# A decoder block's MLP in two sweeps: seven products each for the up and the down projection, factors kept in device memory

## The chip, the cores and the metric

The kernel runs on one core of a Trainium2 chip. The metric is the device time of one launch, in microseconds, as the median of several runs; the profile is one more execution of the same program with the hardware profiler on.

## The reference

One decoder layer on a sequence of 512 tokens, model width 2048, all float32. A first part (delta-rule heads, differential attention, output projection, residual) is the same in both kernels. The change is in the MLP that follows it, cut to what matters:

```python
h = h + jnp.einsum("bse,ed->bsd", mix, w_o[l])
u = rms_norm(h, mlp_norm[l])                                   # 512 x 2048
hid = jnp.square(jax.nn.relu(jnp.einsum("bsd,df->bsf", u, w_up[l])))   # w_up 2048 x 8192
h = h + jnp.einsum("bsf,fd->bsd", hid, w_down[l])              # w_down 8192 x 2048
return rms_norm(h, final_norm)
```

## The kernel before

**Three matmuls for one.** Every float32 operand is split into a high part (rounded to fp32r by ScalarE, line 147 in `parts`) and a low part (the rest, by VectorE, line 149), and a product is the sum of high x high, high x low and low x high. A weight tile of 128 x 1024 elements is one unit: one ScalarE instruction, one VectorE instruction, then TensorE's matmuls. The high and low tiles live in two rings of 3 buffers (`hi`, `lo`), the loaded weights in a ring `raw` of 6.

**Blocks.** The hidden width 8192 is cut in 16 blocks of 512. The up projection of a block is plain: `cols_steps` makes 16 k-steps x 4 column groups x 3 = 192 matmuls of 512 moving columns (lines 204 to 206; block 0 by `up_first`, lines 978 to 980). Its result passes relu and square on ScalarE (lines 965, 966).

**Down in seven products.** The down projection of blocks 0 to 14 is done with Strassen's scheme in Winograd's form on halves of the tokens, of the block's rows and of the output columns: seven products instead of eight. `seven_steps` makes the seven left factors of a block out of the activations (sums, then a split by `two`, 512 elements per partition each); `block_steps` makes the weight sums t1 to t4 in place with VectorE (lines 864, 870, 878, 884), splits them, and calls `product` (lines 835 to 837): 12 matmuls of 512 columns for each of the seven products and each of two column halves `p`, 168 for a block. After every product VectorE adds the PSUM result to the rows of the residual `h`, which stays in SBUF (lines 850, 852). The last block's down projection is plain (192 matmuls).

**Order.** Down of block b is woven with up of block b + 1 and b + 2 and with the factors of block b + 1. The program text is a stream of instructions; a list scheduler of the framework then orders them on each engine, so that an instruction that is ready goes ahead of one that isn't. All weight loads go through SyncE's queue in one chain.

Of the kernel before, what the change touches and what calls it, by code (L numbers as in the profile page):

```python
# [12 lines left out]
F32 = mybir.dt.float32  # L13
F32R = mybir.dt.float32r
AF = mybir.ActivationFunctionType
# [16 lines left out]
def hybrid_block(ctx: ExitStack, tc: tile.TileContext, x, attn_norm, w_in, conv_w, a_log, dt_bias,  # L32
# [758 lines left out]
    weave(chain(attn_values(1, dv[1]), attn_cols(2, df[2]), attn_cols(3, df[3])), att)  # L791


    def half_tile():

        return big("p", [P, 2, 2, 256], nm="hf")

    def two(src):
        z = big("w", [P, 2, 2, 256], F32R, nm="op")
        A.activation(z[:, 0], src, AF.Copy)  # L800
        V.tensor_sub(z[:, 1], src, z[:, 0].bitcast(F32))
        return z[:, 0], z[:, 1]

    def seven_steps(left, f):

        a11, a21, a12, a22 = left[0][:, 0], left[0][:, 1], left[1][:, 0], left[1][:, 1]
        f["a12"] = two(a12)
        yield
        f["a11"] = two(a11)
        z = big("m", [P, 2, 2, 256], nm="s12")  # L810
        s1, s2 = z[:, 0], z[:, 1]
        V.tensor_add(s1, a21, a22)
        yield
        f["s1"] = two(s1)
        V.tensor_sub(s2, s1, a11)
        yield
        f["s2"] = two(s2)
        s4 = s1
        V.tensor_sub(s4, a12, s2)
        yield  # L820
        f["s4"] = two(s4)
        s3 = s2
        V.tensor_sub(s3, a11, a21)
        yield
        f["s3"] = two(s3)
        yield
        f["a22"] = two(a22)
        yield

    def product(bank, fac, wts, first, last_):  # L830
        (ah, al), (bh, bl) = fac, wts
        for k in range(2):
            for t in range(2):
                st = slice(t * P, (t + 1) * P)
                T.matmul(bank[t], lhsT=ah[:, k, st], rhs=bh[:, k, :], start=first and k == 0, stop=False, skip_group_check=True)  # L835
                T.matmul(bank[t], lhsT=ah[:, k, st], rhs=bl[:, k, :], start=False, stop=False, skip_group_check=True)  # L836
                T.matmul(bank[t], lhsT=al[:, k, st], rhs=bh[:, k, :], start=False, stop=last_ and k == 1, skip_group_check=True)  # L837

    def block_steps(f, w, row0, rows):

        for p in range(2):
            def quarter(i, j):
                r0, c0 = row0 + 256 * i, 1024 * j + 512 * p
                return load_w(w[r0:r0 + 256, c0:c0 + 512].rearrange("(k p) n -> p k n", p=P), [P, 2, 512])

            def add(bank, half, cg, op=ALU.add):
                for t in range(2):
                    dst = rows[2 * half + t][cg]
                    if op == ALU.add:
                        V.tensor_add(dst, bank[t], dst)  # L850
                    else:
                        V.tensor_sub(dst, dst, bank[t])

            b21, b11, b12, b22 = quarter(1, 0), quarter(0, 0), quarter(0, 1), quarter(1, 1)
            Y = [bank(), bank()]
            product(Y, f["a12"], parts(b21, 2), True, True)
            add(Y, 0, p)
            yield
            X = [acc(), acc()]
            product(X, f["a11"], parts(b11, 2), True, False)  # L860
            add(X, 0, p)
            yield
            t1 = b11
            V.tensor_sub(t1, b12, b11)
            Z = [acc(), acc()]
            product(Z, f["s1"], parts(t1, 2), True, False)
            add(Z, 1, p + 2)
            yield
            t2 = t1
            V.tensor_sub(t2, b22, t1)  # L870
            product(X, f["s2"], parts(t2, 2), False, False)
            add(X, 0, p + 2)
            yield
            product(Z, f["s4"], parts(b22, 2), False, True)
            add(Z, 0, p + 2)
            yield
            t3 = b12
            V.tensor_sub(t3, b22, b12)
            product(X, f["s3"], parts(t3, 2), False, True)
            add(X, 1, p)  # L880
            add(X, 1, p + 2)
            yield
            t4 = b21
            V.tensor_sub(t4, t2, b21)
            Y = [bank(), bank()]
            product(Y, f["a22"], parts(t4, 2), True, True)
            add(Y, 1, p, ALU.subtract)
            yield


    mixT = {}
# [52 lines left out]
    run(rows_steps(po, w_o[0], 3 * 512, 512, mix, by_token=4, done=finish))  # L944


    def up_unit(u):
# [4 lines left out]
    uT = to_feature_major(h, rstd, g_mlp)  # L952
    NBLK = DFF // 512

    def up_steps(b, j, left):
        z = half_tile()
        for k in range(2):
            po = sps()
            yield from cols_steps(po, w_up[0], (4 * b + 2 * j + k) * P, uT, tag="x")
            squared_relu(z, k, po)  # L960
        left.append(z)

    def squared_relu(z, k, po):
        r = big("m", [P, 512], nm="relu")
        A.activation(r, po, AF.Relu)
        A.activation(z[:, :, k, :], r.rearrange("p (i s) -> p i s", i=2), AF.Square)

    def up_first():

        po = [acc() for _ in range(4)]  # L970
        for u in range(KD // 2):
            hi, lo = up_unit(u) if u else first
            for j in range(2):
                k = 2 * u + j
                ah, al = uT[k]
                for c in range(4):
                    st = slice(c * P, (c + 1) * P)
                    T.matmul(po[c], lhsT=hi[:, j, st], rhs=ah, start=k == 0, stop=False)
                    T.matmul(po[c], lhsT=hi[:, j, st], rhs=al, start=False, stop=False)
                    T.matmul(po[c], lhsT=lo[:, j, st], rhs=ah, start=False, stop=k == KD - 1)  # L980
        for j in range(2):
            z = half_tile()
            for k in range(2):
                squared_relu(z, k, po[2 * j + k])
            lefts[0].append(z)

    def up(b, j):
        return up_steps(b, j, lefts[b]) if b < NBLK else iter(())

    lefts = [[] for _ in range(NBLK)]  # L990
    facs = [{} for _ in range(NBLK)]
    up_first()
    floor.clear()
    run(seven_steps(lefts[0], facs[0]))
    run(up(1, 0))
    for b in range(NBLK - 2):
        down = block_steps(facs[b], w_down[0], 512 * b, h)
        for p in range(2):
            ups = up(b + 1, 1) if p == 0 else up(b + 2, 0)
            fac = seven_steps(lefts[b + 1], facs[b + 1]) if p == 1 else iter(())  # L1000
            for i in range(7):
                next(down)
                next(fac, None)
                if i % 2 == 0:
                    next(ups, None)
            run(ups)


    down = block_steps(facs[NBLK - 2], w_down[0], 512 * (NBLK - 2), h)
    ups = up(NBLK - 1, 1)  # L1010
    for i in range(7):
        next(down)
        if i % 2 == 0:
            next(ups, None)
    run(ups)
    lft = lefts[NBLK - 1]
    fac = [[two(lft[j][:, i]) for i in range(2)] for j in range(2)]
    wts = {}

    def plain_steps(t):  # L1020
        for cg in range(4):
            po = bank()
            for j in range(2):
                if (cg, j) not in wts:
                    r0 = 512 * (NBLK - 1) + 256 * j
                    wts[cg, j] = split(w_down[0, r0:r0 + 256, cg * 512:(cg + 1) * 512].rearrange("(k p) n -> p k n", p=P),
                                       [P, 2, 512], ("u", "u"))
# [83 lines left out]
```

## Time and profile before

| | |
|---|---|
| median of 3 runs | 2282.8 us (2282.29 to 2284.34) |
| the profiled execution's own time | 2282.81 us |
| its span, first to last instruction | 2281.1 us |
| mean granted TensorE clock | 0.997 of full speed |
| one block of the MLP in the steady part | 81.5 us |

The span is the time on the chip from the first to the last instruction; the time of a run has 1.7 us more around it. TensorE matmuls are pipelined: the duration shown for one is longer than the distance to the next one's start, so what a matmul costs in a stream is read from the starts.

### The profile page before, as it was taken

The page shows a single profiled execution, that of the slowest core. Times are in us where ns is not written, and L with a number is a line of the kernel's source. Part 1 is how long each engine was busy: PE and PEld are TensorE (multiplying, and loading weights), DVE is VectorE, ACT ScalarE, POOL GpSimd, SP SyncE. Part 2 cuts the span into 40 slices and gives each one's busy share as a digit, 9 for nine tenths or more (in the row PEclk, how much of TensorE's full clock was granted, in tenths as well). Part 3 has the DMA queues.
Part 4 walks back from the last instruction along what each step waited for, and adds up shares of the span by engine and source line. Part 5 has one row for each costly group of instructions (what it writes and reads, how often), then busy time and mean ns, then how long its engine had stood idle before and what let it go on. Part 6 is the DMA issues. An engine that isn't in the chain of part 4 may idle for free.

```text
span 2281.1 us, 27449 instructions
## 1 busy us (share of the span) xinstructions
PE 2245.4 (98%) x10649; PEld 1864.8 (82%) x10649; DVE 1523.3 (67%) x2338; ACT 887.8 (39%) x1444; POOL 55.5 (2%) x85
## 2 busy tenths in 40 slices
PE   8999999999999999999999999999999999999998
PEld 7988777778888788788888888888888888888887
DVE  5467787863355623437787687777778778777776
ACT  5233434432344523433344343343334334434343
POOL 0000100100000000000000000000000000000000
PEclk9999999999999999999999999999999999999999
DMA  8433333433232434233333333232332333323332
GB/s 282 141 111 95 109 97 96 117 92 110 85 95 88 139 92 151 83 105 98 109 93 119 95 99 113 93 123 90 98 115 93 115 98 95 118 93 120 93 127 95
DMA packets 288570, 249.67 MB, mean 109 GB/s; under 512 B 17300, under 2 KB 229560, under 8 KB 288440
## 3 DMA queue, kind: packets, MB, share of 16 engines
q1 hardware_dynamic: 287952, 247.72, 35.3%
q8 instruction: 83, 1.36, 0.3%
q14 instruction: 47, 0.39, 0.1%
q10 hardware_dynamic: 488, 0.21, 0.0%
HBM read 236.86 MB, written 11.03 MB: 109 GB/s over the span
## 4 chain that ended last, share of the span: by engine, by line
PE 90%; DVE 7%; ACT 1%; issue 1%; DMA 1%; POOL 0%; SPq 0%; ACTq 0%; POOLq 0%; DVEq 0%
PE s L206 10%; PE s L204 10%; PE s L205 10%; PE acc L837 6%; PE acc L836 6%; PE acc L835 6%; PE acc L204 5%; PE acc L205 4%; PE acc L206 4%; PE acc L220 3%; PE acc L221 3%; PE acc L222 3%; PE s L837 2%; PE s L836 2%; PE s L835 2%; DVE X L520 2%
## 5 line engine op out<-in xcount | busy, mean ns | idle before, releaser
L149 DVE TENSOR_TENSOR lo<-raw,hi 128x1024 fp32r<-128x1024 f32 (+2 forms) x370 | 443.9, 1200 | 342.3 <-ACT hi L147 337.5
L147 ACT ACTIVATE hi<-raw 128x1024 fp32r<-128x1024 f32 (+2 forms) x370 | 384.5, 1040 | 674.5 <-PE acc L205 136.7
L204 PE MATMUL s<-u,hi 128*128 128x512 f32 x960 | 373.4, 389 | 0.0
L205 PE MATMUL s<-u,hi 128*128 128x512 f32 x960 | 373.4, 389 | 0.0
L206 PE MATMUL s<-u,lo 128*128 128x512 f32 x960 | 373.4, 389 | 0.0
L149 DVE TENSOR_TENSOR lo<-x,hi 128x1024 fp32r<-128x1024 f32 x120 | 146.7, 1223 | 181.0 <-ACT hi L147 181.0
L204 PE MATMUL acc<-u,hi 128*128 128x512 f32 x640 | 260.6, 407 | 0.8 <-DVE dvl L679 0.6
L205 PE MATMUL acc<-u,hi 128*128 128x512 f32 x640 | 251.6, 393 | 0.0
L206 PE MATMUL acc<-u,lo 128*128 128x512 f32 x640 | 250.7, 392 | 0.0
L147 ACT ACTIVATE hi<-x 128x1024 fp32r<-128x1024 f32 x120 | 127.5, 1062 | 315.0 <-PE s L205 226.2
L836 PE MATMUL acc<-lo,op 128*128 128x512 f32 x600 | 233.4, 389 | 0.0
L837 PE MATMUL acc<-hi,op 128*128 128x512 f32 x600 | 233.4, 389 | 0.0
L835 PE MATMUL acc<-hi,op 128*128 128x512 f32 x600 | 233.1, 389 | 0.0
L850 DVE TENSOR_TENSOR h<-acc,h 128x512 f32<-128x512 f32 x360 | 232.2, 685 | 0.6 <-PE acc L837 0.5
L205 PEld LDWEIGHTS s<-u,hi 128*128 128x128 f32 x960 | 180.2, 188 | 37.4
L206 PEld LDWEIGHTS s<-u,lo 128*128 128x128 f32 x960 | 180.2, 188 | 37.4
L204 PEld LDWEIGHTS s<-u,hi 128*128 128x128 f32 x960 | 180.2, 188 | 37.4
L220 PE MATMUL acc<-hi,u 128*128 128x512 f32 (+2 forms) x384 | 144.7, 379 | 7.6 <-ACT hi L147 5.9
L204 PEld LDWEIGHTS acc<-u,hi 128*128 128x128 f32 x640 | 120.7, 189 | 25.0 <-DVE dvl L679 1.0
L206 PEld LDWEIGHTS acc<-u,lo 128*128 128x128 f32 x640 | 120.4, 188 | 25.3
L221 PE MATMUL acc<-lo,u 128*128 128x512 f32 (+2 forms) x384 | 140.5, 366 | 0.2 <-DVE lo L149 0.2
L222 PE MATMUL acc<-hi,u 128*128 128x512 f32 (+2 forms) x384 | 140.6, 366 | 0.0
(266 smaller groups left out, 3228.2 us busy)
## 6 DMA issues: line engine op xcount, KB each, us to landing
raw<-in_w_down_dram SPq DMA_DIRECT2D x128, 512.0 KB, 5.6
x<-in_w_up_dram SPq DMA_DIRECT2D x120, 512.0 KB, 4.2
raw<-in_w_in_dram SPq DMA_DIRECT2D x96, 512.0 KB, 3.9
raw<-in_w_o_dram SPq DMA_DIRECT2D x32, 512.0 KB, 3.8
raw<-in_w_in_dram SPq DMA_DIRECT2D x16, 384.0 KB, 8.3
w<-in_xt_dram SPq DMA_DIRECT2D x8, 512.0 KB, 8.5
p<-in_x_dram SPq DMA_DIRECT2D x8, 512.0 KB, 10.0
raw<-in_x_dram SPq DMA_DIRECT2D x8, 512.0 KB, 3.6
```

What stands on the lines that cost most here:

```text
L147: A.activation(hi, raw, AF.Copy)
L149: floor["lo"] = V.tensor_sub(lo, raw, hi.bitcast(F32))
L204: T.matmul(po, lhsT=hi[:, j, :], rhs=ah, start=k == 0, stop=False)
L205: T.matmul(po, lhsT=hi[:, j, :], rhs=al, start=False, stop=False)
L206: T.matmul(po, lhsT=lo[:, j, :], rhs=ah, start=False, stop=k == KD - 1)
L220: T.matmul(o, lhsT=ah[:, st], rhs=bh, start=k == 0, stop=False)
L221: T.matmul(o, lhsT=ah[:, st], rhs=bl, start=False, stop=False)
L222: T.matmul(o, lhsT=al[:, st], rhs=bh, start=False, stop=k == KD - 1)
L835: T.matmul(bank[t], lhsT=ah[:, k, st], rhs=bh[:, k, :], start=first and k == 0, stop=False, skip_group_check=True)
L836: T.matmul(bank[t], lhsT=ah[:, k, st], rhs=bl[:, k, :], start=False, stop=False, skip_group_check=True)
L837: T.matmul(bank[t], lhsT=al[:, k, st], rhs=bh[:, k, :], start=False, stop=last_ and k == 1, skip_group_check=True)
L850: V.tensor_add(dst, bank[t], dst)
```

## The change

Up and down become two sweeps. First all 16 blocks are projected up, each of blocks 1 to 15 with seven products too; their down factors are made on the way, and stored to device memory by GpSimd's queue (`keep`). Then the down projection runs over groups of blocks, [0], [1, 2, 3], [4, 5, 6], [7, 8, 9], [10, 11, 12], [13, 14]: the factors of a group are loaded back (`recall`) once and used for both column halves, the blocks of a group accumulate in the same PSUM banks, and the rows of `h` are added to once per product and group. Block 15's down projection stays plain.

- In the up products the weights are the stationary operand and the moving one is a factor of u, 256 columns wide. `u_factors` makes the factors of u once, after `up_first`; for it ScalarE copies each of 16 transposed tiles out of PSUM once more (`uf`).
- `h` is stored to device memory (16 stores on GpSimd's queue) to free its buffers for the factors of u, and loaded back (`rows_back`) at the start of the down sweep.
- The weight sums are made unit by unit beside another product's splits (`sums`, `beside`).
- `raw` has 9 buffers.

```python
-    BUFS = {"p": 10, "x": 2, "w": 8, "m": 2, "u": 16, "raw": 6, "hi": 3, "lo": 3}
+    BUFS = {"p": 10, "x": 2, "w": 8, "m": 2, "u": 16, "raw": 9, "hi": 3, "lo": 3}
...
+    def keep(b, name, src):
+        z = pair_of(src, "w")
+        fscr[b, name] = dp.tile([P, 1024], F32, name=f"f_{name}_{b}")
+        G.dma_start(out=fscr[b, name], in_=z.bitcast(F32).rearrange("p a k s -> p (a k s)"))
...
+    def recall(b, name):
+        z = big("w" if name in ("a12", "a22") else "u", [P, 2, 2, 256], F32R, nm="fac")
+        with tc.issue_after(last_load[0].ins):
+            last_load[0] = nc.sync.dma_start(out=z.bitcast(F32).rearrange("p a k s -> p (a k s)"), in_=fscr[b, name])
+        return z[:, 0], z[:, 1]
+
+    def sums(out, a, b):
+        return [lambda o=o, x1=x1, x2=x2: V.tensor_add(o, x1, x2) for o, x1, x2 in zip(out, a, b)]
...
+        product(X, fa, t1, True, False)                              # block_steps, one group, one p
+        product(Y, fa, t4, True, True, sums(t1, t1, b12))
+        product(Z, fa, t1, True, False, sums(t1, t1, b22))
+        product(X, factor("s2"), t1, False, False)
+        product(Z, factor("s4"), b22, False, True, sums(t4, t4, t1))
+        product(Y, factor("a22"), t4, True, True, sums(b12, b12, b22))
+        product(X, factor("s3"), b12, False, True)
...
+            A.activation(uf[k // 8][k % 8 // 2][:, k % 2], pv, AF.Identity, scale=sc)
+    for cg in range(4):
+        for t in range(NT):
+            G.dma_start(out=hscr[2 * cg + t // 2][:, t % 2, :], in_=h[t][cg])
...
+    def up_product(bank, name, wts, first, last_, beside=()):
+        for n, raw in enumerate(wts):
+            bh, bl = parts(raw, 4)
+            if beside:
+                beside[n]()
+            for j in range(4):
+                k = 4 * n + j
+                ah, al = fu[name][k][:, 0, :], fu[name][k][:, 1, :]
+                for c in range(2):
+                    dst, st = bank[:, c * 256:(c + 1) * 256], slice(c * P, (c + 1) * P)
+                    T.matmul(dst, lhsT=bh[:, j, st], rhs=ah, ...)
+                    T.matmul(dst, lhsT=bh[:, j, st], rhs=al, ...)
+                    T.matmul(dst, lhsT=bl[:, j, st], rhs=ah, ...)
...
+    left = up_first()
+    for b in range(1, NBLK):
+        fac, nxt = seven_steps(b - 1, left), []
+        for _ in up_steps(b, nxt):
+            next(fac, None)
+        run(fac)
+        left = nxt
+    last_fac = four_steps(NBLK - 1, left)
```

`up_steps` of a block makes the seven `up_product`s in the same order as above (a11, a12, s1, s2, s4, a22, s3), with two units per product. Between them ScalarE copies four results out of PSUM (512 elements each), VectorE combines the four quarters of the block (4 instructions of 512), and ScalarE applies relu and square (8 of 512). After each product one step of `seven_steps` of the block before is issued.

## Rows read from the trace of the kernel before

**Rows 1.** The page: the span, and busy time by engine.
```profile
span 2281.1 us, 27449 instructions
PE 2245.4 (98%) x10649; PEld 1864.8 (82%) x10649; DVE 1523.3 (67%) x2338; ACT 887.8 (39%) x1444; POOL 55.5 (2%) x85
```
**Rows 2.** Waits of TensorE from 940 us to the end: total, times, longest.
```profile
PE s L185 <- DVE un L180: 1.2, 1, 1.2
PE s L185 <- ACT un L177: 0.8, 2, 0.5
PE acc L978 <- ACT u L163: 0.3, 1, 0.3
```
**Rows 3.** Windows: one block, two stretches of heavy VectorE, the entry, the kernel's start.
```profile
core 0: us, PE busy (x) PEld busy (x) DVE busy (x) ACT busy (x) POOL busy (x), PEclk, DMA share, GB/s
1600.00:1681.50 81.50, 81.50 (x362) 67.47 (x361) 61.50 (x74) 31.60 (x38) 0.00 (x0) 1.00 0.33 104
...
1641.00:1666.00 25.00, 25.00 (x112) 20.71 (x111) 24.59 (x32) 11.92 (x16) 0.00 (x0) 1.00 0.39 126
...
2160.00:2240.00 80.00, 80.00 (x353) 65.80 (x352) 68.15 (x82) 36.84 (x47) 0.00 (x0) 1.00 0.34 112
...
952.00:964.00 12.00, 10.75 (x70) 8.70 (x71) 9.87 (x20) 11.38 (x21) 0.68 (x1) 1.00 0.16 44
...
20.00:40.00 20.00, 18.49 (x105) 18.17 (x106) 14.39 (x39) 11.69 (x24) 3.03 (x4) 1.00 1.05 391
```
**Rows 4.** Timeline of TensorE: matmuls of 256 columns in attention, of 272, of 512.
```profile
807.06 0.28 PE L734 MATMUL s<-dvl,at 128*128 128x256 f32 x1
...
808.26 0.28 PE L735 MATMUL s<-dvh,at 128*128 128x256 f32 x1
...
87.80 0.29 PE L220 MATMUL acc<-hi,u 128*128 128x272 f32 x1
...
89.94 0.29 PE L222 MATMUL acc<-hi,u 128*128 128x272 f32 x1
...
1704.12 0.39 PE L204 MATMUL s<-u,hi 128*128 128x512 f32 x1
...
1709.33 0.39 PE L206 MATMUL s<-u,lo 128*128 128x512 f32 x1
```
**Rows 5.** Timeline of VectorE, back to back: 1024 elements, and 512.
```profile
1646.93 1.22 DVE L149 TENSOR_TENSOR lo<-raw,hi 128x1024 fp32r<-128x1024 f32 x1
1648.07 1.22 DVE L149 TENSOR_TENSOR lo<-x,hi 128x1024 fp32r<-128x1024 f32 x1
...
1655.28 0.68 DVE L819 TENSOR_TENSOR s<-hf,s 128x512 f32<-128x512 f32 x1
1655.88 1.22 DVE L149 TENSOR_TENSOR lo<-raw,hi 128x1024 fp32r<-128x1024 f32 x1
```
**Rows 6.** The high-part group (by line, ScalarE) in the block of 1600 to 1681.5 us.
```profile
L147 ACT ACTIVATE hi<-raw 128x1024 fp32r<-128x1024 f32 x14 | 14.8, 1057 | 23.0 <-PE s L205 8.3 <-PE acc L837 7.9 <-DVE raw L864 4.9
```
**Rows 7.** Timeline of ScalarE at the MLP's entry.
```profile
954.95 2.40 ACT L163 ACTIVATE u<-s,vec 128x512 fp32r<-128x512 f32 x4
...
964.84 1.12 ACT L147 ACTIVATE hi<-raw 128x1024 fp32r<-128x1024 f32 x1
```
**Rows 8.** DMA issues: KB each, median us to landing.
```profile
raw<-in_w_down_dram SPq DMA_DIRECT2D x128, 512.0 KB, 5.6
...
szscr<-sz SPq DMA_DIRECT2D x4, 512.0 KB, 3.5
```
**Rows 9.** Timelines of GpSimd and VectorE where both work, and one VectorE operation alone.
```profile
165.04 1.40 POOL L460 TENSOR_SCALAR_AFFINE_SELECT pT<-pT 128x1024 f32<-128x1024 f32 x1 [1.63 <-ACT pT L456]
...
164.74 3.02 DVE L415 SCALAR_TENSOR_TENSOR cv<-cv,cw 128x511 f32<-128x511 f32 x3
...
187.94 0.74 DVE L415 SCALAR_TENSOR_TENSOR cv<-cv,cw 128x511 f32<-128x511 f32 x1
```

More of the change, by code (lines that the diff above doesn't have):

```diff
@@ L809, in seven_steps @@
-        f["a11"] = two(a11)
         z = big("m", [P, 2, 2, 256], nm="s12")
         s1, s2 = z[:, 0], z[:, 1]
-        V.tensor_add(s1, a21, a22)
+        keep(b, "a11", a11)
         yield
-        f["s1"] = two(s1)
-        V.tensor_sub(s2, s1, a11)
+        keep(b, "a12", a12)
+        V.tensor_sub(s1, a21, a22)
         yield
-        f["s2"] = two(s2)
-        s4 = s1
-        V.tensor_sub(s4, a12, s2)
+        keep(b, "s1", s1)
+        negated_less(s2, s1, a11)
         yield
-        f["s4"] = two(s4)
@@ L822, in seven_steps @@
-        s3 = s2
-        V.tensor_sub(s3, a11, a21)
+        keep(b, "s2", s2)
         yield
-        f["s3"] = two(s3)
+        negated_less(s1, s2, a12)
+        keep(b, "s4", s1)
         yield
-        f["a22"] = two(a22)
+        keep(b, "a22", a22)
+        V.tensor_add(s2, a11, a21)
         yield
-    def product(bank, fac, wts, first, last_):
-        (ah, al), (bh, bl) = fac, wts
-        for k in range(2):
-            for t in range(2):
[L834 to L888, printed above, removed]
@@ new lines, in seven_steps, with four_steps @@
+        keep(b, "s3", s2)
+        yield
+    def four_steps(b, left):
+        for j in range(2):
+            for i in range(2):
+                keep(b, f"a{i + 1}{j + 1}", left[j][:, i])
+                yield
+    def recall(b, name):
[3 more added lines that the diff above has]
+        return z[:, 0], z[:, 1]
@@ new lines, in sums, with product @@
+    def sums(out, a, b):
+        return [lambda o=o, x1=x1, x2=x2: V.tensor_add(o, x1, x2) for o, x1, x2 in zip(out, a, b)]
+    def product(bank, facs, wts, first, last_, beside=()):
+        for n, ((ah, al), raw) in enumerate(zip(facs, wts)):
+            bh, bl = parts(raw, 2)
+            if beside:
+                beside[n]()
+            for k in range(2):
+                for t in range(2):
+                    st = slice(t * P, (t + 1) * P)
+                    head, tail = first and n == 0 and k == 0, last_ and n == len(facs) - 1 and k == 1
+                    T.matmul(bank[t], lhsT=ah[:, k, st], rhs=bh[:, k, :], start=head, stop=False, skip_group_check=True)
+                    T.matmul(bank[t], lhsT=ah[:, k, st], rhs=bl[:, k, :], start=False, stop=False, skip_group_check=True)
+                    T.matmul(bank[t], lhsT=al[:, k, st], rhs=bh[:, k, :], start=False, stop=tail, skip_group_check=True)
@@ L980, in up_first @@
                     T.matmul(po[c], lhsT=lo[:, j, st], rhs=ah, start=False, stop=k == KD - 1)
+        floor.clear()
+        run(u_factors())
+        left = []
         for j in range(2):
@@ L983, in up_first @@
             for k in range(2):
[L984 to L997, printed above, removed]
-        for p in range(2):
[L999 to L1006, printed above, removed]
@@ L1009, in hybrid_block @@
[L1009 to L1017, printed above, removed]
+                r = big("m", [P, 512], nm="relu")
+                A.activation(r, po[2 * j + k], AF.Relu)
+                A.activation(z[:, :, k, :], r.rearrange("p (i s) -> p i s", i=2), AF.Square)
@@ new lines, in up_first, with u_factors, put @@
+            left.append(z)
+        return left
+    fu = {n: [None] * 8 for n in ("a11", "a12", "a22", "s1", "s2", "s3", "s4")}
+    def u_factors():
+        for q in range(4):
+            xa, xb = uf[0][q], uf[1][q]
+            a11, a21, a12, a22 = xa[:, :, 0, :], xa[:, :, 1, :], xb[:, :, 0, :], xb[:, :, 1, :]
+            z = big("m", [P, 2, 2, 256], nm="s12")
+            s1, s2 = z[:, 0], z[:, 1]
+            def put(n, src, tag):
+                o = big(tag, [P, 2, 2, 256], F32R, nm="u" + n)
+                A.activation(o[:, :, 0, :], src, AF.Copy)
+                V.tensor_sub(o[:, :, 1, :], src, o[:, :, 0, :].bitcast(F32))
+                for i in range(2):
+                    fu[n][2 * q + i] = o[:, i]
+            V.tensor_sub(s1, a21, a22)
+            put("s1", s1, "p")
+            negated_less(s2, s1, a11)
+            put("s2", s2, "p")
+            negated_less(s1, s2, a12)
+            put("s4", s1, "x" if q < 2 else "p")
+            V.tensor_add(a21, a11, a21)
+            for i in range(2):
+                k = 2 * q + i
+                fu["a11"][k], fu["a12"][k], fu["a22"][k] = uh[k][:, 0], uh[8 + k][:, 0], uh[8 + k][:, 1]
+                o = uh[k][:, 1]
+                A.activation(o[:, 0, :], a21[:, i, :], AF.Copy)
+                V.tensor_sub(o[:, 1, :], a21[:, i, :], o[:, 0, :].bitcast(F32))
+                fu["s3"][k] = o
+            yield
@@ new lines, in hybrid_block, with rows_back @@
+    left = up_first()
[6 more added lines that the diff above has]
+    last_fac = four_steps(NBLK - 1, left)
+    hb = []
+    for i in range(8):
+        z = big("p", [P, 2, 512], nm="hb")
+        hb.append(z)
+    h = [[hb[2 * cg + t // 2][:, t % 2, :] for cg in range(4)] for t in range(NT)]
+    def rows_back(cgs):
+        for cg in cgs:
+            for i in range(2):
+                with tc.issue_after(last_load[0].ins):
+                    last_load[0] = nc.sync.dma_start(out=hb[2 * cg + i], in_=hscr[2 * cg + i])
@@ L1018, in hybrid_block @@
+    groups = [[0]] + [[b, b + 1, b + 2] for b in range(1, NBLK - 3, 3)] + [[NBLK - 3, NBLK - 2]]
+    for g in groups:
+        f = {}
+        for p in range(2):
+            down = block_steps(g, f, p, w_down[0], h)
+            if g is groups[0]:
+                rows_back((p, p + 2))
+            if g is groups[-1] and p == 1:
+                break
+            for _ in down:
+                next(last_fac, None)
+    fac = []
     wts = {}
```

158 lines of the change are left out of this document (135 added, 23 removed).

## The prediction

> **What bounds the kernel now.** I read the page's busy times first. TensorE is busy for 2245.4 of 2281.1 us, VectorE for 67% and ScalarE for 39% [rows 1]. Next the waits: from the MLP's entry at 940 us to the end the trace names three kinds of wait of TensorE, 2.3 us together, all at the entry [rows 2]. So the MLP costs what TensorE's stream costs, and only its price moves the end, unless another engine falls behind. Then one block as a window: 81.5 us, TensorE full, VectorE 61.5 (75%), ScalarE 31.6 [rows 3]. A block has 192 up and 168 down matmuls of 512 columns, so one costs 81.5 / 360 = 0.2264 us. The shown duration (0.39) is a latency: 24 starts run from 1704.12 to 1709.33, 0.2265 apart [rows 4]. A reader who multiplies durations gets 0.28 us for a 256-column matmul and a change that costs hundreds of us; the starts say otherwise.
>
> **The change part by part.**
>
> *Up matmuls (the gain).* Plain: 192 x 0.2264 = 43.5 us per block. New: 7 products x 48 = 336 matmuls of 256 columns. The price of one: eleven starts in attention from 807.06 to 808.26 are 0.120 apart; eighteen of 272 columns from 87.80 to 89.94 are 0.1259 apart, a run of a long stage [rows 4]. From 0.2264 at 512 and 0.1259 at 272 the slope is 0.000419 per column, so 256 comes to 0.1192; bounds 0.119 and 0.126. I take 0.120, seen directly: 40.3 us. Gain 3.2 us a block, 15 blocks: 47.5 us (the bounds: 52 to 17). The fixed part, some 13 ns a matmul, paid twice as often, eats 2.3 of the 5.4 us that seven products instead of eight save. Break-even is 43.5 / 336 = 0.1294.
>
> The Trainium skill (TensorE: Matmul & The Clock Gate, "Back-to-back issue gap") puts the warm gap at N / 2.4 + 2.5 ns, 109 ns at 256 columns and 216 at 512; by it the gain would be 15 x (41.4 - 36.7) = 71 us. The rows show 226 at 512, so the measurement decides.
>
> *VectorE in the up sweep.* Distances of starts, back to back: 1.14 us for 1024 elements, 0.60 for 512 [rows 5]. Check on the old block: 22 splits and 8 weight sums of 1024, 43 operations of 512 (32 additions to h, 11 for factors): 34.2 + 25.8 = 60.0, against 61.5 shown [rows 3]. A new up block: 14 splits (16.0), 8 sums (9.1), 4 combinations of quarters (2.4), 11 operations for factors (6.6): 34.1, with the same excess 35. That is 87% of 40.3. It goes in spurts: the steps of a12 and s1 hold 6.4 + 5.8 = 12.1 us against 11.5 of TensorE, and so do s4 and a22; a11, s2, s3 hold 2.9 to 4.1 against 5.7. Two units of 2.9 us stand split ahead, which covers 0.6. Does TensorE keep going at such a load? Yes: 25 us with VectorE busy 24.6, and 80 us at 68.2, with TensorE full and 353 matmuls at 0.2266 in the second [rows 3]. So no charge, but only 5 us a block of cover are left (20 before).
>
> *ScalarE in the up sweep.* 14 high parts at 1.06 or less [rows 6], 7 factors, 4 copies and 8 of relu and square at about 0.55: 24 to 25 us of 40. Hidden.
>
> *Down sweep.* As many matmuls, 168 x 0.2264 = 38.0 us per block. VectorE per group of three and both halves: 42 splits, 24 sums, 32 additions, 94 us of 114. In group [0] the additions aren't shared: 14 splits and 8 sums (25.1), 32 additions (19.2), and four factors of block 15 (2.4): 46.7 against 38.0. Some of the lag is worked off in the next group, which has 20 us to spare: 0 to 9, I take 6.
>
> *Entry.* ScalarE paces the transposes now: 11.38 of 12 us busy, TensorE already short by 1.25 there [rows 3]. The 16 extra copies `uf` at 0.60 [rows 7] are 9.6 us in front of the second weight unit's high part, which came at 964.84, when TensorE had nearly run through the transposes and the first unit. Bounds 0 and 10; I take 8, for the copies stand earlier in the program. Then `u_factors`: 28 operations of 1024 and 8 of 512 on VectorE, 37 us, beside the 43 us of `up_first`, which need 8 of splits; the s1 factors are due 11.5 us after it. Bounds 0 and 12; I take 3.
>
> *Moves.* 105 factors and four of block 15 are stored at 0.5 MB each, h (4 MB) goes out and in, and all factors come back: about 117 MB more. An up block has 4 MB of weights and 3.7 of stores in 40 us, 190 GB/s; the old block runs at 104, the start at 391 over 20 us [rows 3]. A store of this size took 3.5 us to land, a load 5.6 [rows 8], from SyncE's queue; GpSimd's has no row. One store is due every 5.8 us. From 3.5 us (nothing) to about 12 us, where three free `w` buffers no longer cover it, it costs nothing. Behind a store on GpSimd stand only further stores. On SyncE's queue a recall that waits for a `u` buffer holds the weight loads behind it. The worst place is the turn from up to down: some 33 loads of 0.52 MB (17.3 MB) are due in 57 us, 303 GB/s. At 391 that's free, at 300 even; bounds 0 and 15, I take 3.
>
> *The rest.* The tail's weight splits share the `u` ring with recalled factors, and the spurts above may leave gaps: 0 to 15, I take 5. Nine `raw` buffers in the earlier stages: nothing, since TensorE waits for no load there after the start.
>
> *Sum.* -47.5 + 8 + 3 + 6 + 3 + 5 = -22.5 on the execution of span 2281.1: 2258.6, and 1.7 us around it: **2260 us**. That execution (2282.81) is the median run to 0.01 us.
>
> **The rivals.**
>
> *VectorE loses its cover to GpSimd's stores (slower).* In the up sweep each block issues 7 stores from GpSimd, whose work can get in VectorE's way: while GpSimd ran one operation of 1.40 us, three operations of VectorE took 3.02 instead of about 2.1 [rows 9], 0.9 lost. At 0.9 per store VectorE needs 35 + 6.3 = 41.4 a block, just over TensorE; it decides from (5.3 + 22.5 / 15) / 7 = 0.97 us per store. At 1.4 per store, the whole of GpSimd's operation, a block takes 44.8: +4.5 x 15 = 68, **2328 us**. For it: VectorE's load of 87%. Against: a store isn't an elementwise operation, and no row shows what it takes.
>
> The Trainium skill (SBUF — State Buffer, "Who interferes with whom") names this trap: GpSimd's DMAs are written by its cores through a port pair shared with VectorE; it adds that an addition of two SBUF tensors takes only the read side and descriptors the write side, by inference. By the second half this rival falls; no row tests it.
>
> *The entry and the turn eat the gain (same).* Copies 10, `u_factors` 12, turn 15, group [0] 9: 46 of 47.5, **2282 us**. For it: ScalarE's 95% at the entry. Against: all four at their worst.
>
> *Nothing is given back (more gain).* The list scheduler slips the weight splits between the copies, the lag of group [0] is absorbed: 2282.8 - 47.5 + 3, **2238 us**. For it: the old trace has hardly a wait to show.
>
> *The factors' loads come late in every group.* In the first half of a group 10.5 MB of factors and 6 of weights are due in 57 us, 290 GB/s. If the queue gives 250, a group loses some 9 us beyond what was loaded ahead: 4 groups, 36 us on the forecast, 2296. Against: 391 shown, and loads can start in the half before.
>
> **How the numbers follow.** Forecast 0.52, its own range 2245 to 2275. More gain 0.12. Same 0.10. VectorE bound 0.18, of which a part stops between 2262 and 2278. Late loads 0.08. Faster by over 0.2% (below 2278.2; 0.2% is about what this measurement can tell): 0.52 + 0.12 + 0.04 = 0.68. Same: 0.10. Slower: 0.22. The range 2236 to 2308 leaves out about one in ten at each end.
>
> **What would show it.** Right: L-lines of `up_product` start 0.120 us apart in long runs, an up block of about 40.3 us with VectorE near 35 busy, TensorE short of work for about 8 us behind the transposes and a few us at the turn, down groups of three at 114 us. Wrong: VectorE operations longer than 1.22 us while GpSimd stores, TensorE waiting for `lo` in every up block, ScalarE waiting for a `w` buffer behind a store, SyncE's queue stopped in the first half of a group. The prediction fails if the price of 256 columns isn't 0.120 in a stream, or if the up sweep isn't TensorE's.

## The result, and the profile after

The changed kernel takes 2256.2 us, the median of four runs (2254.98 to 2256.91); the kernel before takes 2282.6 beside it. The ratio is 0.9882, 95% interval 0.9865 to 0.9899. The profiled execution after took 2254.98 us and its span is 2253.2, against 2281.1 [rows 1]: 27.9 us less.

The page after, the lines that answer to [rows 1], and the DMA queue that the stores went to (packets, MB, share):

```profile
span 2253.2 us, 32786 instructions
...
PE 2205.4 (98%) x12809; PEld 1929.9 (86%) x12809; DVE 1644.9 (73%) x2356; ACT 1017.2 (45%) x1630; POOL 122.6 (5%) x210
...
q0 software_dynamic: 16976, 61.35, 7.6%
```

TensorE has 2160 matmuls more and is busy 40 us less; every other engine has more to do. The windows after, to be held against [rows 3]: an up block, a down group of three, the entry, the last part of `up_first`, and three stretches from the turn on:

```profile
core 0: us, PE busy (x) PEld busy (x) DVE busy (x) ACT busy (x) POOL busy (x), PEclk, DMA share, GB/s
1013.50:1053.80 40.30, 40.30 (x338) 40.30 (x337) 34.79 (x38) 24.23 (x34) 3.75 (x7) 1.00 0.59 197
1665.00:1779.00 114.00, 114.00 (x505) 94.38 (x503) 98.37 (x100) 44.62 (x42) 0.00 (x0) 1.00 0.68 246
950.00:962.00 12.00, 11.15 (x56) 8.98 (x57) 6.82 (x13) 10.54 (x18) 1.15 (x2) 0.86 0.49 149
986.00:1004.00 18.00, 18.00 (x81) 14.92 (x80) 18.00 (x29) 9.77 (x17) 0.00 (x0) 1.00 0.20 59
...
1609.00:1619.00 10.00, 6.49 (x28) 4.53 (x26) 3.75 (x6) 2.89 (x5) 0.00 (x0) 1.00 0.88 310
1619.00:1650.00 31.00, 25.77 (x98) 18.48 (x99) 30.09 (x37) 11.45 (x13) 1.60 (x3) 0.94 0.88 332
1650.00:1664.00 14.00, 14.00 (x61) 11.34 (x62) 13.71 (x18) 5.84 (x6) 0.00 (x0) 1.00 0.54 165
```

An up block is full of TensorE's work with VectorE at 34.79 of 40.30; a group of three takes its 114 us. Of these stretches the turn is the one that lacks work: in its first 10 us VectorE too is mostly idle (3.75), in the next 31 it has hardly a gap (30.09) while TensorE has 25.77.

The timeline of TensorE in the up sweep, where [rows 4] had the price:

```profile
1099.83 0.28 PE L1097 MATMUL s<-us,hi 128*128 128x256 f32 x1
...
1105.94 0.28 PE L1097 MATMUL acc<-us,hi 128*128 128x256 f32 x1
```

From the first row to the last there are 52 starts, so they are 0.1198 us apart.

TensorE's waits from 930 us to the end, against [rows 2]:

```profile
PE s L867 <- DVE lo L149: 4.6, 3, 3.0
PE acc L867 <- DVE lo L149: 3.3, 2, 2.9
PE acc L866 <- ACT hi L147: 1.6, 2, 1.1
PE s L866 <- DMA fac<-f_a: 1.5, 1, 1.5
PE s L1009 <- DVE un L1004: 1.2, 1, 1.2
PE s L1205 <- ACT u L147: 1.1, 1, 1.1
```

None of these lies in the up sweep. The named waits are not the whole loss, since each is followed by matmuls that start later apart. So the losses of the down sweep are counted from the timeline: for its 2712 matmuls of 512 columns, the distance to the start before, less 0.2264 us, summed over a stretch. Where the span went, by the starts of each stage:

| stage | before | after | difference | charged |
|---|---|---|---|---|
| to the first transpose of the MLP | 952.1 | 950.1 | -2.0 | 0 |
| to the end of `up_first` | 53.0 | 54.2 | +1.2 | +11 |
| up sweep, 15 blocks | 15 x 43.47 | 604.8 (40.32 each) | -47.3 | -47.5 |
| first down group, lost | 0 | 13.5 | +13.5 | +9 |
| rest of the down sweep, lost | 0 | 0.6 and 7.2 in the tail | +7.8 | +5 |
| lost in the old woven blocks and the old tail | 1.8 | 0 | -1.8 | 0 |
| after the last matmul | 8.2 | 8.8 | +0.6 | 0 |

The stages are cut at the first start of each in the two timelines; 15 x 43.47 is 192 x 0.2264, fifteen times; "charged" is what the prediction put down for the stage. The sum is -28.0, against -27.9 of span.

### The profile page after: what moved, and what is told of

The parts are those of the page before. It is cut to its first block, busy times and chain, and to the rows that moved or that the text cites. A ratio compares the mean times of both kernels' runs of the same rounds, so it can differ in the third digit from the quotient of the medians.

```text
span 2253.2 us, 32786 instructions
## 1 busy us (share of the span) xinstructions
PE 2205.4 (98%) x12809; PEld 1929.9 (86%) x12809; DVE 1644.9 (73%) x2356; ACT 1017.2 (45%) x1630; POOL 122.6 (5%) x210
## 4 chain that ended last, share of the span: by engine, by line
PE 89%; DVE 8%; ACT 1%; issue 1%; DMA 1%; POOL 0%; SPq 0%; ACTq 0%; POOLq 0%; DVEq 0%
PE s L1098 5%; PE s L1097 5%; PE s L1096 5%; PE acc L204 5%; PE s L867 5%; PE s L868 5%; PE acc L205 5%; PE s L866 5%; PE acc L206 5%; PE acc L1097 4%; PE acc L1096 4%; PE acc L1098 4%; PE acc L867 4%; PE acc L868 4%; PE acc L866 4%; PE acc L220 3%
## 5 line engine op out<-in xcount | busy, mean ns | idle before, releaser
L147 ACT ACTIVATE hi<-raw 128x1024 fp32r<-128x1024 f32 (+2 forms) x520 | 544.0, 1047 | 796.8 <-PE acc L205 134.6
L149 DVE TENSOR_TENSOR lo<-raw,hi 128x1024 fp32r<-128x1024 f32 (+2 forms) x520 | 624.1, 1205 | 318.4 <-ACT hi L147 306.7
L855 DVE TENSOR_TENSOR raw<-raw,raw 128x1024 f32<-128x1024 f32 x210 | 253.7, 1218 | 8.5 <-DMA raw<-in_w_down_dram 7.1
L867 PE MATMUL s<-lo,fac 128*128 128x512 f32 x480 | 187.6, 391 | 4.6 <-DVE lo L149 4.6
L866 PE MATMUL s<-hi,fac 128*128 128x512 f32 x480 | 187.0, 391 | 2.4 <-DMA fac<-f_a 1.5
L868 PE MATMUL s<-hi,fac 128*128 128x512 f32 x480 | 187.3, 390 | 0.0
L867 PE MATMUL acc<-lo,fac 128*128 128x512 f32 x360 | 140.4, 390 | 3.3 <-DVE lo L149 3.3
L866 PE MATMUL acc<-hi,fac 128*128 128x512 f32 x360 | 139.9, 390 | 2.5 <-ACT hi L147 1.6
L868 PE MATMUL acc<-hi,fac 128*128 128x512 f32 x360 | 140.1, 389 | 0.0
L1098 PE MATMUL acc<-uh,lo 128*128 128x256 f32 x480 | 135.8, 283 | 0.0
L1096 PE MATMUL s<-uh,hi 128*128 128x256 f32 x480 | 135.8, 283 | 0.0
L1097 PE MATMUL s<-uh,hi 128*128 128x256 f32 x480 | 135.8, 283 | 0.0
L1098 PE MATMUL s<-uh,lo 128*128 128x256 f32 x480 | 135.8, 283 | 0.0
## 6 DMA issues: line engine op xcount, KB each, us to landing
fac<-f_s SPq DMA_DIRECT2D x60, 512.0 KB, 10.3
fac<-f_a SPq DMA_DIRECT2D x49, 512.0 KB, 10.2
```

The costliest lines, as they stand in the source:

```text
L147: A.activation(hi, raw, AF.Copy)
L149: floor["lo"] = V.tensor_sub(lo, raw, hi.bitcast(F32))
L855: return [lambda o=o, x1=x1, x2=x2: V.tensor_add(o, x1, x2) for o, x1, x2 in zip(out, a, b)]
L1096: T.matmul(dst, lhsT=bh[:, j, st], rhs=ah, start=head, stop=False, skip_group_check=True)
L1097: T.matmul(dst, lhsT=bh[:, j, st], rhs=al, start=False, stop=False, skip_group_check=True)
L1098: T.matmul(dst, lhsT=bl[:, j, st], rhs=ah, start=False, stop=tail, skip_group_check=True)
```

## The experiments

Each was timed in turn with the kernel before, whose median was 2282.8 to 2283.1 us there. All but one start from the kernel after (2256.2).

### Two sweeps with a plain up projection

```python
     def up_steps(b, left):
         left += [half_tile(), half_tile()]
+        for j in range(2):
+            for k in range(2):
+                po = bank()
+                yield from cols_steps(po, w_up[0], (4 * b + 2 * j + k) * P, uT)
...
-        up_product(X, "a11", t1, True, False)                  # and the six others
...
-        run(u_factors())                                       # nor the copies uf
```

> The two sweeps as in the changed kernel, but blocks 1 to 15 projected up with the plain 192 matmuls of 512 columns; the factors of u and the extra copies are left out. Theory (the gain is the price of TensorE's stream: 43.5 us against 40.3 us a block): 2256 + 15 x 3.15 - 1 at the entry = 2302 us (2296 to 2307), and TensorE without waits in the up sweep. Rival (the gain came from the two sweeps, by fewer additions on VectorE): within 10 us of 2256.

Measured: 2296.6 us (2295.65 to 2301.23), at the lower end of the theory's range; ratio to the kernel before 1.0065 (1.0052 to 1.0079). The window of one up block:

```profile
1100.00:1143.50 43.50, 43.50 (x194) 36.03 (x193) 16.83 (x19) 16.70 (x24) 3.73 (x7) 1.00 0.56 181
```

TensorE is full at 43.50 a block and VectorE at 16.83. So the seven products in the up projection are the whole gain: 48 us in the up sweep, of which 40.4 are left between the two runs. The two sweeps by themselves, with their stores and recalls, cost 13.6 us against the kernel before. The first down group loses 9.1 us here and the tail 7.3; with seven-product up 13.5 and 7.2. So a third of the loss at the turn goes with the seven products of the sweep ahead of it.

### Every factor stored twice

```python
         G.dma_start(out=fscr[b, name], in_=z.bitcast(F32).rearrange("p a k s -> p (a k s)"))
+        twin = dp.tile([P, 1024], F32, name=f"g_{name}_{b}")
+        G.dma_start(out=twin, in_=z.bitcast(F32).rearrange("p a k s -> p (a k s)"))
```

> Every factor is stored twice from GpSimd's queue, the second time to a place nobody reads: 14 stores for an up block. Theory (a store costs GpSimd half a microsecond and VectorE nothing): the same time, 2256 within 4 us; VectorE's operations in the up sweep keep 1.22 us and 35 us a block. Rival (GpSimd's stores take VectorE's time, 0.9 us each): VectorE needs 35 + 6.3 or more a block, above 40.3 us, and the time rises by 15 to 100 us.

Measured: 2265.8 us (2265.19 to 2266.63). The window of one up block:

```profile
1013.50:1053.80 40.30, 40.30 (x338) 40.30 (x337) 34.81 (x38) 24.29 (x33) 7.46 (x14) 1.00 0.79 286
```

VectorE's two largest groups in the up sweep of this run, then of the kernel after:

```profile
L149 DVE TENSOR_TENSOR lo<-raw,hi 128x1024 fp32r<-128x1024 f32 x204 | 247.8, 1221 | 44.1 <-ACT hi L147 43.8 <-PE acc L1099 0.3
L857 DVE TENSOR_TENSOR raw<-raw,raw 128x1024 f32<-128x1024 f32 x115 | 140.1, 1218 | 1.0
```

```profile
L149 DVE TENSOR_TENSOR lo<-raw,hi 128x1024 fp32r<-128x1024 f32 x204 | 247.7, 1220 | 63.4 <-ACT hi L147 63.4
L855 DVE TENSOR_TENSOR raw<-raw,raw 128x1024 f32<-128x1024 f32 x116 | 141.3, 1218 | 1.0
```

TensorE's two largest waits from 1609 to 1660 us, with every store doubled:

```profile
PE s L868 <- DMA fac<-f_a: 5.5, 1, 5.5
PE s L868 <- ACT hi L147: 2.7, 1, 2.7
```

With 14 stores a block instead of 7, VectorE has 34.81 us of work instead of 34.79, and its two kinds of large operation last 1221 and 1218 ns; with 7 they last 1220 and 1218. GpSimd's stores take nothing from VectorE's two-input operations, so the rival on VectorE's cover falls. The 9.6 us that the kernel loses lie outside the theory's range and below the rival's. In the profile 7.5 us of loss are added in the first down group, where a recall is late by 5.5 us: there the stores and the recalls meet. Another 2.8 are added in the up sweep, which takes 607.6 us here against 604.8, by the way of the `w` buffers. The longest wait of ScalarE for a DMA there, and that of VectorE behind it:

```profile
ACT op L802 <- DMA g_s<-op: 29.6, 14, 2.9
DVE op L803 <- ACT op L802: 25.1, 29, 2.3
```

ScalarE stands before the next factor until a second store has read its buffer, VectorE's low parts come later for it, and TensorE waits for some of them (four waits that the trace names, 1.2 us together, and shorter gaps at the same line). This is a sign that the prediction had named (ScalarE waiting for a `w` buffer behind a store); the kernel after has no such wait.

### Stores on SyncE's queue

```python
-        G.dma_start(out=fscr[b, name], in_=z.bitcast(F32).rearrange("p a k s -> p (a k s)"))
+        nc.sync.dma_start(out=fscr[b, name], in_=z.bitcast(F32).rearrange("p a k s -> p (a k s)"))
```

> The factor stores are issued from SyncE's queue, which also issues the weight loads, instead of GpSimd's. Theory (weight loads run ahead of TensorE by several units in the up sweep, and a store waits only for a factor of the step before): 2255 to 2262 us, most of it at the turn, where a late store holds b22 and the recalls. Rival (each store waits for VectorE's low part, and the weight loads behind it are held: TensorE waits for raw weights in every up block, 1 to 4 us a block): 2270 to 2316.

Measured: 2256.5 us (2254.17 to 2257.29), the same as the changed kernel. The largest waits of SyncE's queue in the up sweep:

```profile
SPq L812 <- DVE op L803: 330.9, 101, 22.0
SPq L135 <- DVE lo L149: 141.8, 82, 2.4
```

The queue stands behind late stores for 331 us in all, once for 22, and TensorE waits for nothing there: the weight loads run that far ahead. That the stores are on GpSimd's queue is worth nothing that can be measured here.

### The kernel before with nine `raw` buffers

```python
-    BUFS = {"p": 10, "x": 2, "w": 8, "m": 2, "u": 16, "raw": 6, "hi": 3, "lo": 3}
+    BUFS = {"p": 10, "x": 2, "w": 8, "m": 2, "u": 16, "raw": 9, "hi": 3, "lo": 3}
```

> The kernel before with nine raw buffers for six, nothing else. Theory (the 2 us that the changed kernel is ahead before its MLP come from the longer ring): 2280.6 us, ahead by 2 us at the first transpose of the MLP. Rival (they come from something else, or the ring is lost again in the MLP): 2282.6.

Measured: 2281.6 us (2279.4 to 2282.67), ratio 0.9993 (0.9984 to 1.0002). In its profile the first transpose starts at 950.3 instead of 952.1, as in the kernel after, and the span is 1.0 us shorter. In the profiles of the kernel after and its variants, all with nine buffers, the first transpose starts between 948.7 and 950.6. So a lead goes with the ring, against one profile with six. Here 0.9 us of it is lost again in the next stage, where the granted clock falls at the first transposes and the stretch to the end of `up_first` takes 53.9 us instead of 53.0. In the time of the run the lead can't be told from nothing.

### One more copy of each transposed tile

```python
             A.activation(uf[k // 8][k % 8 // 2][:, k % 2], pv, AF.Identity, scale=sc)
+            A.activation(big("m", [P, 512], nm="spare"), pt, AF.Identity, scale=sc)
```

> One more ScalarE copy of each of the sixteen transposed tiles at the entry, into a spare buffer that nothing reads: 16 x 0.60 = 9.6 us more of ScalarE's work ahead of the first up product. Theory (the entry cost 1.2 us instead of 8 because the weight units' high parts were put between the copies, so ScalarE has slack there): 2256 to 2259 us. Rival (the prediction's step: ScalarE paces the entry, and copies of 9.6 us delay the matmuls by some 8): 2262 to 2266.

Measured: 2262.5 us (2261.83 to 2263.55), 6.3 more; the rival's range, not the theory's. But the place is another than the rival's. The windows of the transposes, of the rest of `up_first`, and of the first up block:

```profile
961.00:985.00 24.00, 24.00 (x125) 19.71 (x124) 13.17 (x19) 24.00 (x42) 0.00 (x0) 1.00 0.21 66
985.00:1004.00 19.00, 18.02 (x79) 14.37 (x77) 18.17 (x31) 13.27 (x24) 0.00 (x0) 1.00 0.26 84
1004.00:1013.00 9.00, 5.54 (x37) 5.00 (x37) 8.92 (x14) 8.52 (x15) 0.00 (x0) 0.94 0.00 0
```

While ScalarE is busy without a gap (24.00 of 24), TensorE is full too; from the first transpose to the end of `up_first` it takes 54.9 us, against 54.2. The loss comes behind that, in the first up block, where both splitting engines are full and TensorE has 5.54 of 9 us (part of that stretch at a lower clock, 0.94). What carries it there is `u_factors`. Its first and last operation on VectorE, in the kernel after and then in this run:

```profile
969.87 0.69 DVE L1068 TENSOR_TENSOR s<-uf,uf 128x512 f32<-128x512 f32 x1 [0.24 <-ACT uf L1017]
...
1000.43 0.41 DVE L1080 TENSOR_TENSOR uh<-uf,uh 128x256 fp32r<-128x256 f32 x1
```

```profile
985.37 0.69 DVE L1069 TENSOR_TENSOR s<-uf,uf 128x512 f32<-128x512 f32 x1 [1.92 <-ACT spare L1018]
...
1009.85 0.42 DVE L1081 TENSOR_TENSOR uh<-uf,uh 128x256 fp32r<-128x256 f32 x1
```

In the kernel after these operations end before `up_first` does, with VectorE full (18.00 of 18 us). With 16 more copies they start 15.5 us later and end 9.4 us later, among the splits of the first up block. So ScalarE's lag is carried through `up_first`, which needs little of it, and comes due at the next heavy user; the change itself left 3.5 us of room there, from 1000.8 to 1004.3 us.

### The first recalls from another ring, and the load moved ahead

```python
# first of the two: ring u for the first group's a12 and a22
-        z = big("w" if name in ("a12", "a22") else "u", [P, 2, 2, 256], F32R, nm="fac")
+        z = big("w" if name in ("a12", "a22") and b not in groups[0] else "u", [P, 2, 2, 256], F32R, nm="fac")
# second: this too
+        if bs == groups[0]:
+            b22 = quarter(1, 1)
         fa = factor("a12")
...
-        b22 = quarter(1, 1)
+        if bs != groups[0]:
+            b22 = quarter(1, 1)
```

> In the first down group the recalls of the factors a12 and a22 take a buffer of ring u instead of ring w; all else is the changed kernel (2256.2 us). Theory (the turn loses its 13 us because SyncE's queue stands behind a recall that waits 8.6 us for a w buffer, and the load of b22 behind it comes late): the recall then waits only for u buffers that the last up products let go, b22's load starts up to 8 us sooner, and 5 to 8 us come back: 2248 to 2251 us, with the idle time of TensorE ahead of its first lo operands falling from 7.9 to under 3 us. Rival 1 (the u ring is as late as the w ring, since its buffers hold the up sweep's factors until the last product): 2255 to 2259. Rival 2 (VectorE's own work in a group of one block, more than TensorE's 40.3 us, is what is lost): 2254 to 2257, with VectorE busy without gaps from 1609 to 1650.

> As the run with the recalls in ring u, and the load of b22 is moved ahead of the recall of a12 in the first group. Theory (order of SyncE's queue at the turn): b22 no longer stands behind any recall of a12, so 7 to 9 us of the 13 come back: 2247 to 2249 us, and VectorE's first sum with b22 no longer waits for a DMA. Rival 1 (the buffer of the recall itself is late, so the order does not matter): same as the other run within 1.5 us. Rival 2 (VectorE's work in a group of one): 2254 to 2257.

The 40.3 us that some expectations set beside VectorE's work in a down group are the up block's; a down block has 38.0 us of TensorE's work.

The reason to try them stood in the profile after. SyncE's queue by its timeline, then VectorE's, at the turn:

```profile
1599.40 0.41 SPq L135 DMA_DIRECT2D raw<-in_w_down_dram  x1
1608.62 0.34 SPq L850 DMA_DIRECT2D fac<-f_a  x1
1609.01 0.55 SPq L135 DMA_DIRECT2D raw<-in_w_down_dram  x1
...
1615.25 1.23 DVE L855 TENSOR_TENSOR raw<-raw,raw 128x1024 f32<-128x1024 f32 x1 [6.63 <-DMA raw<-in_w_down_dram]
1616.39 0.69 DVE L1147 TENSOR_TENSOR hf<-acc,e 128x512 f32<-128x512 f32 x1
...
1618.79 1.21 DVE L149 TENSOR_TENSOR lo<-raw,hi 128x1024 fp32r<-128x1024 f32 x1
```

Nothing is issued from 1599.8 to 1608.6: a recall waits 8.6 us for a `w` buffer that a factor store still reads. Behind it stands the load of b22, and VectorE sits 6.63 us in front of the first sum with it, with the last block's combinations and splits queued behind. It looks like the cause of the loss.

Measured: 2254.55 us (2251.98 to 2256.72) and 2254.57 (2253.46 to 2255.05). By its median the first can't be told from the kernel after; but two of its four executions took 2252.0 and 2252.6 us (mean granted clock 0.998 and 0.996), the others 2256.5 and 2256.7 (0.995 and 0.993), and its profile is of the longest. The second is 1.7 us below the kernel after by the medians. The windows of the second at the turn:

```profile
1608.00:1618.00 10.00, 8.68 (x39) 6.58 (x37) 8.50 (x11) 5.70 (x9) 0.53 (x1) 1.00 1.03 419
1618.00:1650.00 32.00, 25.04 (x99) 17.80 (x100) 29.86 (x36) 9.48 (x10) 1.07 (x2) 1.00 0.77 302
```

VectorE now works in the first 10 us too (8.50), and yet TensorE is short of work for the next 32 as before: 11.5 us are lost, against 13.5. With the wait taken away VectorE's own load sets most of the pace (38.4 of 42 us); the queue as it was blocked falls as the cause of most of the loss. Two limits of this reading: about 1 us of the 13.5 is five matmuls 0.43 us apart at a lower clock, which this run doesn't have, and the queue isn't free here either: from 1606.2 to 1614.7 the four loads of `h` stand in it, with the DMA engines full (share 1.03), and VectorE still waits 3.5 us for weights by 1660 us, against 6.9 in the kernel after.

### Groups of one, and the first two blocks in one group

```python
-    groups = [[0]] + [[b, b + 1, b + 2] for b in range(1, NBLK - 3, 3)] + [[NBLK - 3, NBLK - 2]]
+    groups = [[b] for b in range(NBLK - 1)]                                       # first run
+    groups = [[0, 1], [2, 3, 4], [5, 6, 7], [8, 9, 10], [11, 12], [13, 14]]       # second run
```

> Every block of the down sweep is a group of its own, so the rows of h are added to for each block. Theory (VectorE's additions bound a group of one: 25.1 + 19.2 = 44.3 us against 38.0 of TensorE): 14 more such blocks lose 6.3 each, 2256 + 88 = 2344 us (2325 to 2360). Rival (the loss of the first group was late loads alone and the additions hide): 2256 to 2270.

Measured: 2367.1 us (2366.53 to 2367.7), above the range. A window of the down sweep, and below it TensorE's two largest waits from 1610 us to the end:

```profile
1700.00:1800.00 100.00, 88.28 (x367) 67.18 (x366) 97.34 (x118) 30.93 (x30) 0.00 (x0) 1.00 0.50 173
```

```profile
PE s L867 <- DVE lo L149: 58.8, 44, 3.0
PE acc L866 <- DVE hb L888: 12.2, 14, 0.9
```

VectorE is the bound, 97.34 of 100 us. Fourteen blocks were moved into groups of one, 110.9 / 14 = 7.9 us each.

> The down sweep's groups are [0,1], then three of three, then [11,12] and [13,14], instead of [0], four of three and [13,14]. Theory (a group of one has 44 us of VectorE's work beside 40.3 of TensorE's, a group of two less than TensorE's; what the turn loses beyond its late load goes): 4 to 6 us come back: 2250 to 2252 us. Rival 1 (the whole loss is the blocked queue at the turn, and it blocks as long with two blocks): 2255 to 2258. Rival 2 (two more recalls at the turn wait for buffers, and the queue stands longer): 2259 to 2264.

Measured: 2250.1 us (2248.93 to 2250.58), 6.1 below the kernel after. The first group loses 4.5 us and the rest up to the tail 3.7, together 8.2 against 14.1. SyncE's queue is stopped in this run as long as before (8.4 us for the store), and DMA runs at 413 GB/s in the first 10 us. So some four tenths of the loss go with the group of one, with the queue as it was.

### The tail's buffers

```python
-                                       [P, 2, 512], ("x", "x") if cg == 3 and j else ("u", "u"))
+                                       [P, 2, 512], {(0, 0): ("p", "p"), (0, 1): ("w", "w"), (3, 1): ("x", "x")}.get((cg, j), ("u", "u")))
```

> In the tail the split operands of the plain last block take buffers of rings p and w for its first column group and x for its last, instead of ring u for nearly all. Theory (about 3 of the tail's 6 us are TensorE waiting for splits whose buffers come free late): 2252 to 2254 us, with the waits for hi and lo operands after 2190 us gone or halved. Rival (the splits are late because their raw weights or VectorE are late, not their buffers): 2255.5 to 2257.

The timeline of ScalarE, then of TensorE, in the tail of the kernel after:

```profile
2187.64 1.06 ACT L147 ACTIVATE u<-raw 128x1024 fp32r<-128x1024 f32 x1 [2.89 <-PE s L868]
...
2190.66 1.06 ACT L147 ACTIVATE hi<-raw 128x1024 fp32r<-128x1024 f32 x1
...
2199.19 1.06 ACT L147 ACTIVATE u<-raw 128x1024 fp32r<-128x1024 f32 x1 [4.16 <-PE acc L868]
...
2191.77 0.50 PE L866 MATMUL acc<-hi,fac 128*128 128x512 f32 x1 [1.15 <-ACT hi L147]
2196.59 0.50 PE L867 MATMUL acc<-lo,fac 128*128 128x512 f32 x1 [2.95 <-DVE lo L149]
2200.30 0.73 PE L1205 MATMUL s<-u,fac 128*128 128x512 f32 x2 [1.15 <-ACT u L147]
```

A split into ring `u` waits 2.89 and 4.16 us for a product's last matmul (line 868), which reads the recalled factors in that ring. The next high part stands behind it on ScalarE, and the low part behind that on VectorE.

Measured: 2247.9 us (2247.06 to 2249.59), 8.3 below the kernel after and more than the 2 to 4 expected. No wait of TensorE is left after 2140 us, and the tail loses 0.4 instead of 7.2.

### Both together, and groups of three only

```python
+    groups = [[0, 1], [2, 3, 4], [5, 6, 7], [8, 9, 10], [11, 12], [13, 14]]       # first run, with the tail's buffers
+    groups = [[b, b + 1, b + 2] for b in range(0, NBLK - 1, 3)]                   # second run, with the tail's buffers
```

> The changed kernel (2256.2 us) with both edits that gave time back: the tail's buffers (2247.9 alone) and the groups [0,1], three of three, [11,12], [13,14] (2250.1 alone). Theory (the losses lie in two places, the first down group and the tail, and are independent): 8.3 + 6.1 come back, 2240.5 to 2243.5 us, TensorE's idle time ahead of the tail gone. Rival (the tail is paid for by the same buffers or queue as the groups, so the gains overlap): 2244.5 to 2248.

Measured: 2243.5 us (2242.68 to 2244.95), ratio to the kernel before 0.9828 (0.9813 to 0.9843): the fastest of all, 12.7 below the kernel after, where independent losses would give 14.4; that is just at the upper end of the theory's range. In its profile the tail loses 0.3 and the rest 9.5.

> As the run with the tail's buffers, and the down sweep in five groups of three, [0,1,2] to [12,13,14]: no group of one or two is left. Theory (a group loses what VectorE's work a block exceeds TensorE's 40.3 us, and a group of three has 32.5 of 38 us a block, so the turn's late loads are worked off under cover): at most 3 us of the 13.5 at the turn remain, and [12,13,14] covers its own losses: 2236 to 2241 us. Rival 1 (more recalls at the turn: three blocks' factors and weights, 9.4 MB, due before the first product of each kind, so TensorE waits for DMA there): 2244 to 2250. Rival 2 (the wider last group takes the buffers that the tail's splits need): 2242 to 2248 with waits of TensorE after 2150 us.

Measured: 2250.7 us (2249.72 to 2253.42), above the theory's range. TensorE's waits of this run from 1600 us:

```profile
PE s L866 <- DMA fac<-f_a: 5.5, 1, 5.5
PE s L1205 <- ACT p L147: 3.9, 1, 3.9
```

Both rivals hold a part. The turn still loses 8.1 us, most of it one recall that lands 5.5 us late; and the tail loses 9.8, first behind a weight load that ScalarE waited 9.87 us for. A wider group saves VectorE's additions and asks for more loads and buffers at once.

## Why the prediction was right, point by point

**The sum.** The gain was right in size and in cause, and the sum came near in part by luck: on the span 22.5 us less were forecast and 27.9 measured, and the terms between them were off by more, against each other. The entry was charged 9.8 too much; the turn with group [0] 4.5 and the tail with the gaps 2.8 too little; the lead ahead of the MLP (2.0) and the loss of the old blocks (1.8) weren't counted.

**Up matmuls.** The term carried the result: 40.32 us a block, against 40.3 forecast, and -47.3 against -47.5 (the prediction's own factors give 47.2). The distance of starts (0.1198) and not the duration shown (0.28) was the price. By the formula that the Trainium skill (TensorE: Matmul & The Clock Gate, "Back-to-back issue gap") gives for the isolated warm gap it would be 0.109; the trace shows 0.1198, and the measurement decides.

**VectorE in the up sweep.** 34.79 us of the forecast 35, ScalarE 24.23 of 24 to 25, no wait of TensorE in 15 blocks. The rival on GpSimd's stores falls by the run with every store doubled. The Trainium skill (SBUF — State Buffer, "Who interferes with whom") says by inference that an addition of two SBUF tensors shouldn't suffer from GpSimd's DMAs; these runs agree: the additions last 1218 ns with 7 and with 14 stores a block.

**Entry: mis-sized.** Charged 8 + 3, it cost 1.2. The step that failed is "in front of the second weight unit's high part", with 8 taken "for the copies stand earlier in the program": the scheduler issued the first two high parts at 952.24, ahead of the copies, and at 956.60, between them, and TensorE had matmuls of `up_first` to run meanwhile. The 1.2 has two parts. In six profiles of variants with the same entry and a granted clock of 1.00 there, the stretch takes 53.7 to 53.8 us, against 53.0 in the kernel before and in the run with plain up, which has no copies: 0.8 goes with the copies and `u_factors`. The other 0.4 goes with the clock, which fell there in the kernel after and in three variants, each at 54.2: in 950 to 962 us the granted clock was 0.86, six transposes from 952.38 show 1.54 us instead of 0.88, and four matmuls from 953.90 took 1.87 instead of 4 x 0.2264 = 0.91. ScalarE's 95% was a backlog, not a bound; a delay of the size that the prediction feared comes only with another 9.6 us of copies. `u_factors` has 28 operations of 512 elements and 8 of 256, not of 1024 and 512: about 22 us of VectorE, not 37.

**Group [0] and the turn: right kind, too small.** Charged 6 + 3, lost 13.5. The surplus of VectorE in a group of one was worked out as 46.7 - 38.0 = 8.7, cut to 6 for lag worked off later. Where no lighter group follows, a group of one costs 7.9; put together with block 1 it gives back 5.9 of lost time, so the 6 holds. It is the 3 for the turn that was too small: 6 to 8 us are left for it. With plain up the first group loses 9.1 in all, so some 4.4 go with the seven products ahead of it; of the blocked queue, which the prediction named as a danger, only 2 us came back in a profile, about half of them by the clock.

**The rest.** Charged 5 for tail and gaps, lost 7.2 + 0.6, less 1.8 that the old blocks and tail lost; the cause is the `u` ring that the prediction named, as the buffer run shows. Nine `raw` buffers were charged nothing, and go with a lead of 2.0 us.

**The other rivals.** The loads weren't late in every group: the groups of three take their 114 us with 246 GB/s. The two cases at the ends (the entry and the turn eat the gain, and nothing is given back) each had one half: the turn and the tail took 21 us, the entry 1.

What stays open is how the remainder at the turn, beyond VectorE's work in a group of one, divides between late loads (the DMA share is 0.88 to 1.03 in the first 10 us), stores that hold buffers and the backlog from the up sweep; no run takes the one away without the others.

## What to carry to other kernels

Price a matmul by the distance of starts in a stream of its own size; that one number carried the whole gain here. A busy engine in front of a stage is only a cost if what it delays is due before its backlog is worked off: look for what TensorE has to run in the meantime, and for the next heavy user behind it. A large wait in a queue at a seam may hide a bound next to it: take the wait away before calling it the cause, and look at the groups and rings of the first and last pass, where the steady part's cover is missing.

## What the runs showed of the hardware

- A factor store of 0.5 MB on GpSimd's queue shows 0.53 us of GpSimd's time (3.75 us for 7) and lands 3.2 and 4.9 us after issue (medians of 49 and of 60 stores), against 3.0 and 5.1 from SyncE's queue.
- DMA reaches 413 to 419 GB/s over 10 us at the turn, against 391 in [rows 3]; a recall takes 10.2 to 10.3 us to land (medians of 49 and 60), against 7.3 for a weight load of the down projection in this kernel and 5.6 in [rows 8].
- After a pause of TensorE at the turn of the kernel after, matmuls start 0.43 us apart from 1621.67 to 1623.38, the 1.2 GHz level, with a granted clock of 0.94 over 31 us; the run with the recalls and the load moved had 1.00 over the like stretch and lost 11.5 us of 13.5, so the clock isn't most of what the turn costs.
